# Mixer stage of a hybrid decoder layer written in another order: attention ahead of the values and state scans

## The chip, the cores and the metric

The kernel runs on one core of a Trainium2 chip. The time is the device time of one execution in microseconds (us). A core has five engines that follow their own instruction lists and wait for one another: TensorE (PE, with its weight loads as PEld), VectorE (DVE), ScalarE (ACT), GpSimd (POOL) and SyncE (SP), which here only issues DMAs.

## The reference, cut to what matters

512 tokens of width 1024 pass through a SwiGLU block, a mixer and a second SwiGLU block, all in float32, each with a norm ahead and behind. The change is in the mixer:

```python
proj = rms_norm(x, mix_pre_g) @ w_in          # q, k, v, u: 512 columns each
# attention: 4 heads, 2 components of 64, value width 128, causal
p = softmax(where(causal, q @ k.T * 64 ** -0.5, -inf))     # per head and component
o_att = rms_norm((p[0] - lam * p[1]) @ v, sub_g) * (1 - lam_init)
# state space: 32 groups of 16 channels, 64 complex states each
states = associative_scan(a_bar, b_bar @ u)   # along the 512 tokens
y = c_re @ states.real - c_im @ states.imag + d * u
g = gelu(y)
o_ssm = rms_norm(g * sigmoid(g @ w_glu + b_glu), norm_g)
x = x + rms_norm(concat(o_att, o_ssm) @ w_out, mix_post_g)
```

## The kernel before

**Products.** A float32 product is made of three matmuls of 128x128 by 128x512 (`mm3`, L150 to L152). Each weight tile is loaded by SP into `raw`, rounded by ACT into a high half `wh` (L125), and subtracted into a low half `wl` on DVE, or in this stage on POOL (L126). The tiles `raw`, `wh` and `wl` lie in a few slots that are used in turn, so the load of a later tile waits until an earlier one's low half is made.

**The mixer.** After the first SwiGLU block the inputs u of the state space are projected (`ps_u`), then query and key of head 0 (`ps_q`, `ps_k`). The states (`ssm_states`, L737 to L766) work on four blocks of eight groups: PE makes `ps_s`, DVE rotates it (`tcos`, `tsin`), POOL adds (`z`), DVE scans `z` along 64 chunks of 8 tokens (`w`), DVE and POOL rotate back (`wcos`, `wsin`), and DVE adds into `xt`. The outputs (`ssm_outputs`, L776 and L780) multiply the loaded tables `om` and `mm` with `xt` and `u` into `ps_y`, and ACT takes its gelu into `g`. The gate (`glu`) multiplies `g` with `w_glu`, whose weights are two tiles.

**Attention.** A query is split into halves (L854, L855), a key likewise (ACT L865 and L866, DVE L867, once for each of two components). Then for each block of 128 queries: scores of both components (`ps_sc`, L878 to L880; each is 128 queries by 128 to 512 keys), their maxima on DVE (`mx`), exp on ACT (`att`, L883), the difference of both on DVE, transposes back (`ps_at`, L895, copied by ACT L897), the product with the values (`ps_o`, L904), a norm (`att_n`, L915: ACT L167, DVE L160, POOL L161, DVE), and transposes (`ps_ot`, L925) into the operand of the output product. `ps_at`, `ps_ot`, `ps_y` and other small tiles share two banks of the accumulator memory, so a `ps_at` can wait for a gelu that empties its bank.

**Order.** Within the mixer PE's order is that of the code; the other engines are ordered by a scheduler at build time, and each works through its list in order. Before the attention loop the kernel writes the outputs' loads, head 0's projections, the four state blocks and the values in this order:

```python
    ssm_load_outputs()
    drain(att_query(0, xn))
    drain(att_key(0, xn))
    for b in range(4):
        ssm_states(b)
    att_values(xn)
```

The loop `attention(fill)` goes over 4 heads of 4 blocks and takes pieces of other work from the generator `fill` between its steps, as much as `HEAD_PADS` and `PADS` say. There `fill` gives the other heads' projections merged with the state space's outputs and gate (`LENS` are the lengths by which the two streams are kept level), then the first 28 steps of the output product `acc` (`w_out`).

## Time and profile before

| | |
|---|---|
| median of 3 runs | 988.95 us (987.87 to 989.09) |
| span of the profiled execution | 988.8 us |
| its own time beside the span | nothing lies around the span that a row shows: the median is 0.15 us above it |
| PE busy | 956.1 us (97%) |
| mixer, from the first `ps_u` to the last `acc` | 393 to 620 us |
| mean granted clock of TensorE | 0.990 |

The profile is one execution. A wait is put down to the instruction that released it. A granted clock of 1.00 is TensorE's level of 2.4 GHz, 0.50 that of 1.2 GHz; a stretch at 0.50 counts as busy though its matmuls take twice as long, so the busy share alone does not show it.

### The profile page before, as it was taken

To read this page: it belongs to the slowest core of one execution; us is meant where nothing else is said; L and a number is where in the kernel's file an instruction comes from. 1 tells how busy PE (TensorE), PEld (TensorE's weight loads), DVE (VectorE), ACT (ScalarE), POOL (GpSimd) and SP (SyncE) were. 2 spreads that over 40 slices of the span, in tenths; PEclk is the share of its full clock that TensorE was granted. 3 is DMA by queue.
4 is the path that set the end of the run, shared out by engine and by line. 5 is a ranking of instruction groups with operands and counts; after the bars stand their busy time and mean duration, and the time that the engine had idled before them with its cause. 6 is when DMAs were issued, how large, how long until landed. Compare 5 with 4: busy or idle time off the path is not lost.

```text
span 988.8 us, 12741 instructions
## 1 busy us (share of the span) xinstructions
PE 956.1 (97%) x4931; PEld 791.5 (80%) x4931; DVE 471.4 (48%) x946; ACT 339.4 (34%) x567; POOL 157.3 (16%) x216
## 2 busy tenths in 40 slices
PE   5999999999999999998899899999999999999997
PEld 4988777788888888986677677988888888888886
DVE  5599877633331325447467657623333333322323
ACT  5423333323221334222577545522223232312221
POOL 2105333100000033236234315000000000000000
PEclk9999999999999999999899899999999999999999
DMA  7535543533323261596211205322333333232312
GB/s 226 166 92 153 163 131 109 152 97 95 107 86 107 86 192 50 212 195 141 65 43 43 86 23 169 107 64 86 107 87 104 93 99 104 88 107 85 107 43 86
DMA packets 146172, 107.70 MB, mean 109 GB/s; under 512 B 15568, under 2 KB 126704, under 8 KB 145344
## 3 DMA queue, kind: packets, MB, share of 16 engines
q1 hardware_dynamic: 143776, 100.93, 34.8%
q0 software_dynamic: 1184, 3.87, 1.4%
q10 hardware_dynamic: 1152, 2.10, 0.6%
q8 instruction: 39, 0.64, 0.3%
q14 instruction: 21, 0.17, 0.1%
HBM read 97.99 MB, written 8.88 MB: 108 GB/s over the span
## 4 chain that ended last, share of the span: by engine, by line
PE 48%; ACT 1%; DVE 1%; issue 1%; DMA 1%; POOL 0%; DVEq 0%; POOLq 0%; ACTq 0%
PE ps_gu L152 8%; PE ps_gu L150 8%; PE ps_gu L151 8%; PE acc L152 5%; PE acc L150 5%; PE acc L151 5%; PE ps_sc L879 1%; PE ps_o L904 1%; PE ps_sc L878 1%; PE ps_y L776 1%; PE ps_k L150 1%; PE ps_sc L880 1%; DMA raw<-in_ff_w_gate_dram 1%; PE ps_k L151 0%; PE ps_q L150 0%
## 5 line engine op out<-in xcount | busy, mean ns | idle before, releaser
L125 ACT CAST wh<-raw 128x1024 fp32r<-128x1024 f32 x150 | 157.7, 1053 | 448.5 <-issue 152.9
L126 DVE TENSOR_TENSOR wl<-raw,wh 128x1024 fp32r<-128x1024 f32 x132 | 164.1, 1246 | 249.2 <-ACT wh L125 245.1
L150 PE MATMUL ps_gu<-xn_hi,wh 128*128 128x512 f32 (+1 forms) x696 | 265.3, 382 | 0.0
L151 PE MATMUL ps_gu<-xn_lo,wh 128*128 128x512 f32 (+1 forms) x696 | 265.2, 381 | 0.0
L152 PE MATMUL ps_gu<-xn_hi,wl 128*128 128x512 f32 (+1 forms) x696 | 264.9, 381 | 0.0
L150 PEld LDWEIGHTS ps_gu<-xn_hi,wh 128*128 128x128 f32 x696 | 130.8, 188 | 25.4 <-issue 0.8
L152 PEld LDWEIGHTS ps_gu<-xn_hi,wl 128*128 128x128 f32 x696 | 130.8, 188 | 25.0
L151 PEld LDWEIGHTS ps_gu<-xn_lo,wh 128*128 128x128 f32 x696 | 131.0, 188 | 24.7
L150 PE MATMUL acc<-wh,h 128*128 128x512 f32 x352 | 136.9, 389 | 0.0
L151 PE MATMUL acc<-wl,h 128*128 128x512 f32 x352 | 136.9, 389 | 0.0
L152 PE MATMUL acc<-wh,h 128*128 128x512 f32 x352 | 136.1, 389 | 0.0
L319 DVE TENSOR_TENSOR hf<-sg,ps_gu 128x512 f32<-128x512 f32 x44 | 30.2, 686 | 105.8 <-PE ps_gu L152 105.1
L150 PEld LDWEIGHTS acc<-wh,h 128*128 128x128 f32 x352 | 66.1, 188 | 13.8
L152 PEld LDWEIGHTS acc<-wh,h 128*128 128x128 f32 x352 | 66.1, 188 | 13.6
L151 PEld LDWEIGHTS acc<-wl,h 128*128 128x128 f32 x352 | 66.1, 188 | 13.6
L281 POOL TENSOR_SCALAR ss<-ss_post 128x1 f32<-128x1 f32 x12 | 2.6, 213 | 457.8 <-ACT junk_post L167 457.8
L126 POOL TENSOR_TENSOR wl<-raw,wh 128x1024 fp32r<-128x1024 f32 x18 | 44.1, 2456 | 52.8 <-ACT wh L125 52.7
L321 ACT CAST h<-hf 128x512 fp32r<-128x512 f32 x44 | 27.3, 621 | 36.6 <-DVE hf L319 30.0
L322 DVE TENSOR_TENSOR h<-hf,h 128x512 fp32r<-128x512 f32 x44 | 30.1, 684 | 1.4 <-ACT h L321 1.4
L190 PE MATMUL ps_xn<-ident,xs 128*128 128x128 f32 x96 | 14.9, 299 | 13.7 <-DVE xs L185 12.1
L167 ACT ACTIVATE junk_post<-acc 128x512 bf16<-128x512 f32 x24 | 14.3, 596 | 40.1 <-PE acc L152 39.9
L317 ACT ACTIVATE sg<-ps_gu 128x512 f32<-128x512 f32 x44 | 25.8, 587 | 1.5 <-PE ps_gu L152 1.5
(283 smaller groups left out, 1220.4 us busy)
## 6 DMA issues: line engine op xcount, KB each, us to landing
raw<-in_ff_w_gate_dram SPq DMA_DIRECT2D x44, 512.0 KB, 3.9
raw<-in_ff_w_up_dram SPq DMA_DIRECT2D x44, 512.0 KB, 3.9
raw<-in_ff_w_down_dram SPq DMA_DIRECT2D x44, 512.0 KB, 3.3
raw<-in_w_in_dram SPq DMA_DIRECT2D x16, 512.0 KB, 4.1
raw<-in_w_out_dram SPq DMA_DIRECT2D x8, 512.0 KB, 3.3
im_d<-itca SPq DMA_DIRECT2D x4, 512.0 KB, 5.0
om_d<-taps SPq DMA_DIRECT2D x4, 512.0 KB, 3.7
im<-im_d SPq DMA_DIRECT2D x2, 1024.0 KB, 10.2
```

The lines of the kernel that those rows point to most:

```text
L125: act.copy(wh, raw)
L126: eng.tensor_tensor(wl, raw, wh.bitcast(F32), ALU.subtract)
L150: pe.matmul(ps, a[0], b[0], start=start, stop=False)
L151: pe.matmul(ps, a[0], b[1], start=False, stop=False)
L152: pe.matmul(ps, a[1], b[0], start=False, stop=stop)
L167: sum_sq.ins = act.activation(into, src, AF.Square, scale=scale, accum_out=s).ins
L190: pe.transpose(ps[:, k * P:(k + 1) * P], xs[h][:, k * P:(k + 1) * P], ident)
L317: act.activation(sg, ps_g, AF.Silu)
L319: dve.tensor_tensor(hf, sg, ps_u, ALU.mult)
L321: act.copy(hi, hf)
L322: dve.tensor_tensor(lo, hf, hi.bitcast(F32), ALU.subtract)
L776: pe.matmul(ps[par * 64:par * 64 + 64, g * 64:(g + 1) * 64], lhs, rhs[:, g, par], start=(g == n == 0), stop=(g == 7 and n == 1), skip_grou ...
```

## The change

The outputs' loads, the values and the state blocks move into `fill`: the values (now token block by token block, `ps_v`, in place of a product that keeps all four token blocks open) are merged with the states, then come the outputs' loads, head 1's projections, and heads 2 and 3 merged with the outputs and the gate. The first scores are issued right behind key 0. A scan runs over four groups at once, with a `decay` tile (made by ACT, and zeroed by POOL at each group's first chunk) as its factor: 8 scans of 128x256 in place of 32 of 128x64. The last head's blocks go from the longest to the shortest. A pad that overshoots is now carried on to the next. Two scratch tiles for norm sums become one, and comments go, so lines move by 2 to 9.

```diff
-PADS = (2.4, 0.8, 0, 1.65)
+PADS = (0.7, 0.3, 0, 1.65)
-LENS = (31.2, 26.4)
-HEAD_PADS = (2.05, 0.85, 1.0, 0.6)
+LENS = (21.8, 4.6, 20.8, 26.4)
+HEAD_PADS = (9.1, 5.2, 5.2, 5.0)
...
+        decay = small.tile([P, 4, NC], F32, tag="decay", name="decay", bufs=1)
+        act.copy(decay, S.r8[:, gs].unsqueeze(2).broadcast_to([P, 4, NC]))
+        pool.memset(decay[:, :, 0:1], 0.0)
         for ri in range(2):
-            for g in range(4):
-                cs = slice(g * NC, (g + 1) * NC)
-                dve.tensor_tensor_scan(w[:, ri, cs], S.r8[:, blk * 4 + g:blk * 4 + g + 1].broadcast_to([P, NC]),
-                                       z[:, ri, cs], 0.0, ALU.mult, ALU.add)
+            dve.tensor_tensor_scan(w[:, ri, :], decay.rearrange("p g c -> p (g c)"), z[:, ri, :], 0.0,
+                                   ALU.mult, ALU.add)
...
     def att_values(xn):
-        A.v = page([P, NT, HEADS * VD], F32, "v")
...
-        drain(row_steps(xn.get, w_in, KD, 1024, outer(KD, 2), keep_v))
...
+        for t in range(NT):
+            ps = bank("acc", "ps_v")
+            for f in range(KD):
+                hi, lo = xn.get(f, t * P, (t + 1) * P)
+                wh, wl = (w[:, f % 2, :] for w in units[f // 2])
+                mm3(ps, (hi, lo), (wh, wl), f == 0, f == KD - 1)
+                yield 0.68
+            act.copy(A.v[:, t, :], ps)
+            A.v_ready.add(t)
...
     def attention(fill):
+        due = [0.0]
+
         def pad(us):
-            while us > 0:
+            due[0] += us
+            while due[0] > 0:
                 cost = next(fill, None)
                 if cost is None:
                     return
-                us -= cost
-
-        blocks = [(h, i) for h in range(HEADS) for i in range(NT)]
+                due[0] -= cost
+
+        blocks = [(h, i) for h in range(HEADS) for i in (range(NT) if h < HEADS - 1 else reversed(range(NT)))]
...
-    ssm_load_outputs()
+    att_start()
     drain(att_query(0, xn))
     drain(att_key(0, xn))
-    for b in range(4):
-        ssm_states(b)
-    att_values(xn)
...
+    def ssm_first():
+        for b in range(4):
+            ssm_states(b)
+            yield 0.9
+        ssm_load_outputs()
...
     def fill():
-        yield from merged((LENS[0], projections()), (LENS[1], ssm_rest()))
+        yield from merged((LENS[0], att_values(xn), 0.0), (LENS[1], ssm_first(), 0.2))
+        yield from projections((1,))
+        yield from merged((LENS[2], projections(range(2, HEADS)), 0.0), (LENS[3], ssm_rest(), 0.0))
```

What the change makes of the engines' lists is shown at three places. The first is PE behind the last product of key 0 (`ps_k`); before, the first state block and the values (`acc`) stand there:

```order
L150 MATMUL ps_k_3590<-xn_hi,wh 128x512
L151 MATMUL ps_k_3590<-xn_lo,wh 128x512
L152 MATMUL ps_k_3590<-xn_hi,wl 128x512
L737 MATMUL ps_s<-u,im 64x64 x32
L150 MATMUL acc<-wh,xn_hi 128x512
L151 MATMUL acc<-wl,xn_hi 128x512
```

With the change the scores of block 0 (both components) stand directly behind the key's last matmul, and the values (`ps_v`) behind them:

```order
L152 MATMUL ps_k_3571<-xn_hi,wl 128x512
L887 MATMUL ps_sc<-k,q 128x256
L888 MATMUL ps_sc<-k,q 128x256
L889 LDWEIGHTS identb
L889 MATMUL ps_sc<-cmask,identb 128x128
L887 MATMUL ps_sc<-k,q 128x256
L888 MATMUL ps_sc<-k,q 128x256
```

Moved: the scores of head 0's first block are ahead of the values and of every state block.

The second is SP's list of DMAs from the inputs u of the state space on. Before, it reads:

```order
L726 DMA u<-ud 16x16x64 x8
L700 DMA om<-om_d 128x2048
L705 DMA mm<-kd 16x16x128
L726 DMA u<-ud 16x16x64 x8
L705 DMA mm<-kd 16x16x128 x7
L700 DMA om<-om_d 128x2048
L705 DMA mm<-kd 16x16x128 x8
L138 DMA raw<-in_w_in_dram 128x8x128
L138 DMA raw<-in_ssm_w_glu_dram 128x2x512 x2
```

With the change three weight loads of `w_in` and the first of the gate's stand ahead of the tables, and the gate's second behind them:

```order
L726 DMA u<-ud 16x16x64 x16
L138 DMA raw<-in_w_in_dram 128x8x128 x3
L138 DMA raw<-in_ssm_w_glu_dram 128x2x512
L700 DMA om<-om_d 128x2048
L705 DMA mm<-kd 16x16x128 x8
L700 DMA om<-om_d 128x2048
L705 DMA mm<-kd 16x16x128 x8
L138 DMA raw<-in_ssm_w_glu_dram 128x2x512
```

Moved: the tables `om` and `mm`, from between the loads of u to behind four weight loads, and one gate load from beside the other to behind all tables.

The third is PE at the end of the last head. With the change its last three blocks stand there, block 2 of 4, then block 1, then block 0, `acc` being steps of the output product:

```order
L150 MATMUL acc<-wh,o_att 128x512
L151 MATMUL acc<-wl,o_att 128x512
L152 MATMUL acc<-wh,o_att 128x512
L904 MATMUL ps_at<-ident,att 128x128 x2
L934 MATMUL ps_ot<-ident,att_n 128x128
L913 MATMUL ps_o<-v,att 128x128 x2
L904 MATMUL ps_at<-ident,att 128x128
L934 MATMUL ps_ot<-ident,att_n 128x128
L913 MATMUL ps_o<-v,att 128x128
L934 MATMUL ps_ot<-ident,att_n 128x128
L150 MATMUL acc<-wh,o_att 128x512
```

Before, the last transposes (`ps_ot`) of that head have steps of the output product ahead of them and behind them that need only the state space (`o_ssm`):

```order
L925 MATMUL ps_ot<-ident,att_n 128x128
L904 MATMUL ps_o<-v,att 128x128 x4
L150 MATMUL acc<-wh,o_att 128x512
L151 MATMUL acc<-wl,o_att 128x512
L152 MATMUL acc<-wh,o_att 128x512
L150 MATMUL acc<-wh,o_att 128x512
L151 MATMUL acc<-wl,o_att 128x512
L152 MATMUL acc<-wh,o_att 128x512
L150 MATMUL acc<-wh,o_ssm 128x512
L151 MATMUL acc<-wl,o_ssm 128x512
L152 MATMUL acc<-wh,o_ssm 128x512
L925 MATMUL ps_ot<-ident,att_n 128x128
```

Moved: the steps of the output product that stood between the last two blocks now stand ahead of them.

## Rows read from the trace of the kernel before

**Rows 1.** The page's first part: busy time of each engine, share, instructions.
```profile
PE 956.1 (97%) x4931; PEld 791.5 (80%) x4931; DVE 471.4 (48%) x946; ACT 339.4 (34%) x567; POOL 157.3 (16%) x216
```

**Rows 2.** PE's waits at 421 to 590 us: total us, times, longest.
```profile
PE ps_sc L878 <- DVE tsin L746: 3.2, 1, 3.2
PE ps_sc L878 <- ACT att L883: 2.9, 1, 2.9
PE ps_sc L879 <- DVE k L867: 0.8, 1, 0.8
PE ps_o L904 <- ACT att L897: 0.8, 1, 0.8
```

**Rows 3.** The same view for 393 to 421 us.
```profile
PE ps_xn L190 <- DVE rinv_post L158: 1.5, 1, 1.5
```

**Rows 4.** Busy time by stretch; last three columns: clock, DMA share, GB/s.
```profile
463.30:466.70 3.40, 3.40 (x36) 2.60 (x35) 2.91 (x5) 0.00 (x0) 2.77 (x2) 0.50 0.03 7
...
562.20:565.70 3.50, 3.50 (x10) 2.67 (x10) 1.55 (x6) 0.46 (x2) 0.32 (x2) 0.51 0.17 64
```

**Rows 5.** The same columns while om and mm are loaded.
```profile
432.00:446.00 14.00, 14.00 (x170) 11.58 (x171) 12.50 (x30) 5.22 (x8) 7.06 (x8) 1.00 1.00 179
```

**Rows 6.** The timeline behind key 0: start, duration, engine, line, operation.
```profile
430.22 0.39 PE L152 MATMUL ps_k<-xn_hi,wl 128*128 128x512 f32 x1
...
431.58 0.39 PE L152 MATMUL ps_k<-xn_hi,wl 128*128 128x512 f32 x1
431.83 1.04 ACT L125 CAST wh<-raw 128x1024 fp32r<-128x1024 f32 x1 [4.39 <-PE ps_k L151]
...
435.14 0.68 DVE L867 TENSOR_TENSOR k<-ps_k,k 64x512 fp32r<-64x512 f32 x1
```

**Rows 7.** The timeline behind key 3.
```profile
556.13 0.40 PE L152 MATMUL ps_k<-xn_hi,wl 128*128 128x512 f32 x1
...
561.69 0.38 PE L879 MATMUL ps_sc<-k,q 64*128 64x256 f32 x1 [0.84 <-DVE k L867]
```

**Rows 8.** The state work by tile: durations min/median/max in ns.
```profile
L754 DVE TENSOR_TENSOR_SCAN w<-r,z x32: 256/260/2431, 436.6 to 467.2; 128x64 f32<-128x64 f32 x32
...
L746 DVE TENSOR_TENSOR tsin<-ps_s,phases x4: 681/681/692, 433.7 to 461.5; 128x512 f32<-128x512 f32 x4
...
L748 POOL TENSOR_TENSOR z<-tcos,tsin x4: 731/737/771, 435.3 to 462.3; 128x256 f32<-128x256 f32 x4
...
L759 POOL TENSOR_TENSOR wsin<-w,phases x4: 1273/1724/1749, 438.2 to 467.6; 128x512 f32<-128x512 f32 x4
...
L765 DVE TENSOR_TENSOR xt<-wcos,wsin x8: 402/418/2636, 441.3 to 472.3; 64x252 f32<-64x252 f32 x8
```

**Rows 9.** The maxima of the scores at two widths: busy us, mean ns.
```profile
L882 DVE TENSOR_REDUCE mx<-ps_sc 128x1 f32<-128x512 f32 x8 | 5.4, 687 | 1.9 <-PE ps_sc L880 1.8
...
L882 DVE TENSOR_REDUCE mx<-ps_sc 128x1 f32<-128x128 f32 x8 | 2.1, 288 | 2.5 <-PE ps_sc L880 2.5
```

**Rows 10.** SP's issue of the mm tables in the timeline.
```profile
437.56 8.69 SPq L705 DMA_DIRECT2D mm<-kd  x8
```

**Rows 11.** DMA issues at 385 to 500 us: size, median us to landing.
```profile
om<-om_d SPq DMA_DIRECT2D x2, 1024.0 KB, 9.0
mm<-kd SPq DMA_DIRECT2D x16, 128.0 KB, 8.3
...
raw<-in_ssm_w_glu_dram SPq DMA_DIRECT2D x2, 512.0 KB, 8.4
```

**Rows 12.** The timeline behind a block's last product in head 3.
```profile
586.87 0.28 ACT L167 ACTIVATE junk_post<-ps_o 128x128 bf16<-128x128 f32 x1 [0.68 <-PE ps_o L904]
...
588.70 0.27 PE L925 MATMUL ps_ot<-ident,att_n 128*128 128x128 f32 x1
```

**Rows 13.** The low halves of weights on POOL, and gelu on ACT, by tile.
```profile
L126 POOL TENSOR_TENSOR wl<-raw,wh x18: 2364/2393/2835, 389.1 to 557.5; 128x1024 fp32r<-128x1024 f32 x18
...
L780 ACT ACTIVATE g<-ps_y x4: 597/598/598, 475.6 to 492.6; 128x512 f32<-128x512 f32 x4
```

More of the change, by code (lines that the diff above doesn't have):

```diff
@@ L95, in hybrid_layer @@
     make_causal_mask(nc, cmask, MASK)
-    junk = {tag: const.tile([P, 512], BF16, name=f"junk_{tag}") for tag in ("pre", "post")}
+    junk = const.tile([P, 512], BF16, name="junk")
     mhalf = const.tile([P, 1], F32, name="mhalf")
@@ L165, in sum_sq @@
         s = tiny(1, f"ss_{tag}", bufs=4)
-        into = junk["pre" if tag[:3] == "pre" else "post"][:, 0:src.shape[1]]
+        into = junk[:, 0:src.shape[1]]
         sum_sq.ins = act.activation(into, src, AF.Square, scale=scale, accum_out=s).ins
@@ L832, in hybrid_layer, with att_start @@
     A.q, A.k, A.pg, A.po, A.on, A.pq = {}, {}, {}, {}, {}, {}
-    def att_values(xn):
-        A.v = page([P, NT, HEADS * VD], F32, "v")
-        def keep_v(t, ps):
-            act.copy(A.v[:, t, :], ps)
-        drain(row_steps(xn.get, w_in, KD, 1024, outer(KD, 2), keep_v))
+    def att_start():
         A.sub = const.tile([P, VD], F32, name="subln")
@@ L844, in att_values @@
         dve.tensor_scalar(A.sub, A.sub, 1.0 - LAM_INIT, None, ALU.mult)
-        A.o, A.out = [], set()
+        A.o, A.out, A.v_ready, A.done = [], set(), set(), {h: 0 for h in range(HEADS)}
+        A.v = page([P, NT, HEADS * VD], F32, "v")
+    def att_values(xn):
+        units = [weights(w_in[0, j * 256:(j + 1) * 256, 1024:1536].rearrange("(f p) c -> p f c", p=P), [P, 2, 512])
+                 for j in range(KD // 2)]
+        for t in range(NT):
[7 more added lines that the diff above has]
+            A.v_ready.add(t)
     def att_query(h, xn):
@@ L898, in att_mix @@
         yield
-        if i == 0:
+        if h not in A.po:
             A.po[h] = bank("acc", "ps_o")
@@ L907, in att_norm @@
     def att_norm(h, i):
-        if i == 0:
+        if h not in A.on:
             A.on[h] = scratch([P, SEQ], F32, "att_n")
@@ L919, in att_out @@
             A.pq[h] = bank(name="ps_ot")
-        if h % 2 == 0 and blocks[0] == 0:
+        if len(A.o) == h // 2:
             A.o.append(page([P, 2, 2, SEQ], F32R, "o_att"))
@@ L925, in att_out @@
             pe.transpose(A.pq[h][:, vs], A.on[h][:, vs], ident)
-        if blocks[-1] == NT - 1:
+        A.done[h] += len(blocks)
+        if A.done[h] == NT:
             A.out.add(h)
@@ L933, in merged @@
     def merged(*streams):
-        at = [0.0] * len(streams)
+        at = [s[2] for s in streams]
         live = set(range(len(streams)))
@@ L967, in attention @@
                 pad(hp * PADS[1])
+                while i not in A.v_ready:
+                    next(fill)
                 for o in out_due:
@@ L1050, in __getitem__, with projections @@
             return w_out[b, r0:r0 + 256, cols]
-    def projections():
-        for h in range(1, HEADS):
+    def projections(heads):
+        for h in heads:
             yield from att_query(h, xn)
             yield from att_key(h, xn)
+    def ssm_first():
[3 more added lines that the diff above has]
+        ssm_load_outputs()
     def ssm_rest():
```

## The prediction

> **What bounds the kernel now.** The page comes first: PE is busy 956.1 us, 97% of the span [rows 1], so a change can pay only where PE waits or runs slowly, or cost where it makes PE do so. The second view is that of PE's waits in the stretches that the change touches. From 421 us to the end of attention PE waits 3.2 us for `tsin`, the second rotation of the last state block, 2.9 us for an exp, and twice 0.8 us behind key 3 [rows 2]; a small transposing step at 396 us waits 1.5 us for a norm [rows 3]. These make 9.2 us. The third view is the granted clock by stretch. It falls to 0.50, the 1.2 GHz level, in four stretches, of which the first and the last are shown [rows 4]; their lengths are 3.4, 6.9, 3.5 and 3.5 us, 17.3 us at half speed, so some 8.6 us are lost in them. Each followed waits of about 1 to 3 us. All that the change could win is thus about 18 us, half of it only if the clock stays up.
>
> **What the change takes away.** The 3.2 us for `tsin` went because the scores of head 0 stood behind all values and met the last state block's work on DVE; in the new order three of four blocks' work lies under the values. The 2.9 us for exp has the same root. The two waits of 0.8 us behind key 3 fall away as such and come back below in another size. At 396 us the new order gives the norm more products to hide under, so I take the 1.5 us as gained too. Sum: 9.2 us.
>
> **The scans.** The scan of 128x64 takes 0.26 us [rows 8], so a 128x256 costs at most four of these, 1.04 us. From below, DVE's maxima take 687 ns at 512 columns and 288 ns at 128 [rows 9], 1.04 ns a column; 192 more columns add 0.20 us, 0.46 us in all. I take 0.7 us; eight of them make 5.6 us in place of 8.3 us. Nearly all of it is off PE's path. [...] No row of before shows a long scan. [...] The four copies that make `decay` go to ACT and four small memsets to POOL, where there is idle time; they cost nothing unless that cover goes, and then some 0.6 us each, the nearest row being a key cast of half a microsecond's size.
>
> **New wait A: scores right behind key 0.** Before, a state block and the values covered the splitting of the key. Now PE's last key matmul is followed by the scores. In the trace the last key matmul starts at 431.58, ACT rounds a weight tile first (431.83, 1.04 us), and the first DVE low half only starts at 435.14, a cast of the query having been between [rows 6]. Behind key 3 the same chain for both components is seen in full: from the last key matmul at 556.13 to the scores that end it at 561.69 plus 0.38 are 5.9 us, with a copy of about half a microsecond between [rows 7], so 5.4 us. PE has 0.23 us of the key and 1.3 us of scores to do in that time: 3.8 us of wait. Bounds: 3 to 4.4 us.
>
> **Waits K1, K2, K3: scores behind keys 1 to 3.** In the new order only three, six and three matmuls (0.68 to 1.36 us; six matmuls start within 1.36 us [rows 6]) stand between a key and its first scores. For key 1 no weight cast is ahead: 5.4 less 1.04, less 0.23, 0.68 and 1.3 leaves 2.2 us. Key 2 has the cast ahead and six matmuls: 5.4 less 2.9, 2.5 us. Key 3 has the cast and three matmuls, and longer scores: 2.7 us. Together 7.4 us; bounds 5 to 10.
>
> **Wait E: the state chain.** DVE's list now runs the blocks strictly after one another: the rotation of block 1 stands behind the four `xt` of block 0, and the scores of block 2 wait on PE for the bank that `tsin` of state block 2 empties. One turn is two rotations (1.36 us), two `z` (1.48), a scan (0.7), `wsin` (1.5 to 1.72) and four `xt` (1.7) [rows 8], some 6.9 us. PE begins the values at zero, the first block's `tsin` ends at 7.2, the third's at about 21.5. PE gets there at 18.7 (59 matmuls, three `ps_s`, the scores). That is 3 us; bounds 1.5 with the fast scan to 4.5 with the slow one and POOL's longest `wsin`.
>
> **Wait G: the second gate tile.** SP's tables moved. The load of the first gate tile waits for a slot that POOL frees with the low half of key 1's weights, at about 33 us on the same scale (PE has reached the last quarter of the values, then 1.05 us of cast and two low halves of 2.39 us [rows 13]). Only then come `om`, eight `mm`, `om`, eight `mm`. Eight `mm` took SP 8.69 us [rows 10] while the DMA engines were busy all the time [rows 5]: the sixteen take 17.4 us, to about 51. The second gate tile is behind them and landed 8.4 us after issue before [rows 11], so it lands at about 59; bounds 55 and 60. ACT's list has its cast between two exps, and POOL's has its low half ahead of the last state block's `z`. The gelu of the first outputs waits for that block's `wcos` and `wsin`, since `g` is laid into the memory of the phases that they read. So the gelu ends a cast (1.05), a low half (2.39), two `z` (1.48), a scan (0.7), a `wsin` (1.72) and 0.6 us of gelu [rows 8, 13] later, 8 us: at 63 to 68. PE needs the gelu's bank for the transposes of head 0's last block. It is there at 56 if the clock stays up, at about 61 if waits A, E and K1 each bring a half-speed stretch of 3.4 us like those of before. Hence 2 to 12 us; I take 7. Behind the waiting cast on ACT stand the second exp of head 1's first block and all gelus, and PE waits for those next.
>
> **Tail T.** The last head's two shortest blocks now stand at the end with no step of the output product between them. The norm from a block's last product to its transposes takes 1.83 us (586.87 to 588.70) [rows 12]. The end is a copy (0.5), a norm, transposes, another norm, and the halves of the last transposes before the output product can go on, since its next step needs token block 0: 0.5 plus 1.8 plus 1.8 plus some 0.6. That is 4.5 us (bounds 3 to 5.5) where before steps of the output product lay between.
>
> **Sum.** 3.8 + 7.4 + 3.0 + 7 + 4.5 = 25.7 us of new waits, less 9.2 gained: 16.5 us. The half-speed time I leave as it is, 8.6 us: new waits of 2 to 7 us are no shorter than those that it followed before. From the profiled 988.8 us, 0.15 us under the median, this gives **1005 us**; the bounds of the terms reach from 996 to 1015.
>
> **Rivals.** *G and E vanish.* If the tables' load keeps up, because less else loads beside it, and the state chain is shorter, the sum is 15.7 less 9.2: 995 us (990 to 996). For it: the first gate tile and three weights no longer share the DMA with the tables at the same moment. Against: the DMA share of 1.00 [rows 5].
> *Faster, by the clock.* The granted clock stays at 2.4 GHz through the new waits. That gives back 8.6 us, so the kernel is faster as soon as the new waits sum to under 17.8 us, which they do without G and with E or K a little smaller: 15.7 less 17.8 is -2, some 986 us. For it: the wait in the tail of before, under a microsecond, brought no half-speed stretch. Against: four longer ones did [rows 4].
> *Waits only move.* New and old waits balance, 989 us: then A and K would have to cost a third of what key 3's chain shows [rows 7].
> *More half-speed time.* Each new wait of over 2 us brings a stretch and G is at its long end: 1018 us.
>
> **How the numbers follow.** The forecast has a chance of 0.50. G and E vanish: 0.19. Faster: 0.17. Balance within 0.2%, about what a measurement of this kernel can tell from no change: 0.06. More half-speed time: 0.08. Slower is thus 0.77. The range from 986 to 1016 us leaves out the far ends of the last rival and of the faster one.
>
> **What the profile after would show.** PE waiting for `k` (the low halves) behind each key, 2 to 4 us each; for `tsin` once, some 3 us; for the gelu `g` at a `ps_at`, with the second gate tile landing late and ACT waiting for its DMA; for `att_n` at the end of head 3, twice. The 1.5 us at 396 us gone. I would be wrong if the key waits are under 1.5 us each, if the gelu wait is absent, or if no stretch of the mixer is at 1.2 GHz.

## The result, and the profile after

The changed kernel takes **1042.74 us** (four runs, 1041.62 to 1047.65) against 988.68 us of the kernel before measured beside it (987.87 to 989.09): a ratio of 1.0553 [1.0525, 1.0582]. It is 54 us slower. The prediction was 1005 us with a range of 986 to 1016: the sign was right, the size not. The profiled execution has a span of 1041.3 us, 52.5 us more than before.

First the page: the first line answers to [rows 1], the others are PE's busy tenths and its granted clock in 40 slices of 26 us.

```profile
PE 974.4 (94%) x4931; PEld 802.7 (77%) x4931; DVE 466.0 (45%) x922; ACT 341.2 (33%) x571; POOL 157.4 (15%) x220
...
PE   6999999999999998889399797999999999999997
...
PEclk9999999999999999989799898999999999999999
```

PE has the same 4931 matmuls, but is busy 18 us longer, and the span has grown by three times that. Both the busy tenths and the clock dip in slices 16 to 25, the mixer. So the loss has two parts: time in which PE stands still, and time in which it runs at half speed. The stretch view separates them. The next two rows are the mixer from 385 us to where the second SwiGLU block begins, after and then before (PE busy, PEld, DVE, ACT, POOL, granted clock, DMA share, GB/s).

```profile
385.00:673.00 288.00, 239.18 (x1439) 188.10 (x1438) 136.61 (x270) 120.74 (x267) 88.90 (x88) 0.89 0.30 79
```

```profile
385.00:621.00 236.00, 223.80 (x1453) 179.32 (x1453) 142.81 (x296) 120.09 (x265) 88.85 (x85) 0.96 0.39 105
```

PE idles 48.8 us (288 less 239.18) in place of 12.2. Busy time times one less the clock, summed over stretches of 1 us each, gives what half speed costs: 23.2 us in place of 8.3. That is 36.6 and 14.9 us more, 51.5 in all. The way from 385 us to the first matmul of the second SwiGLU block is 52.5 us longer (to 672.9 in place of 620.4), which is the whole loss of the span: outside this stage nothing changed.

What a clock of 0.50 means is in PE's rows: a 128x512 matmul of `ps_v` starts every 0.427 us at 440.1 to 444.0 us, at 0.50, and every 0.23 us at 445.1 to 446.0 us, at 1.00. That is 1.9 times as long and not twice, so the reckoning by the clock puts the loss a little high. By columns, 512 in 0.427 us are 1.2 per ns at 0.50; at 1.00 256 more of them cost 0.107 us (0.227 us for 512 in `ps_k` [rows 6], 0.120 us for 256 in the `ps_u` of before), 2.4 per ns. Levels of 1.2 and 2.4 GHz are an estimate from these rows, if a column is one cycle.

Where PE idles, the chain of waits says by name (393 to 680 us; total us, times, longest). It answers to [rows 2] and [rows 3].

```profile
PE ps_at L904 <- ACT g L782: 14.2, 1, 14.2
PE ps_sc L887 <- ACT k L875: 7.2, 8, 2.1
PE ps_sc L887 <- DVE rinv_att L160: 4.6, 1, 4.6
PE ps_u L150 <- ACT xn_hi L193: 4.3, 1, 4.3
PE ps_z L150 <- DVE q L864: 4.2, 1, 4.2
PE ps_ot L934 <- DVE att_n L924: 3.4, 2, 1.7
PE ps_os L823 <- DVE og L819: 2.6, 1, 2.6
PE ps_sc L888 <- DVE k L876: 2.6, 8, 0.5
PE ps_gt L798 <- ACT g L782: 1.3, 1, 1.3
```

None of the waits of [rows 2] and [rows 3] is left in its place; the 1.2 us for an exp stand at 631 us, in the last head. The predicted ones are all here: `g` (G), `k` in sixteen pieces (A and K), `att_n` twice (T), and one of 4.6 us (E). Two things were not predicted: 4.3 us for `xn_hi` at the very start, where a gain was expected, and the gate's waits (`ps_z`, `ps_os`, `ps_gt`), 9.1 us in all with one of 1.0 for `gl`.

**Behind key 0** (answers to [rows 6]):

```profile
433.39 0.39 PE L152 MATMUL ps_k<-xn_hi,wl 128*128 128x512 f32 x1
435.92 0.39 PE L887 MATMUL ps_sc<-k,q 128*128 128x256 f32 x1 [2.14 <-ACT k L875]
436.64 0.38 PE L888 MATMUL ps_sc<-k,q 64*128 64x256 f32 x1 [0.33 <-DVE k L876]
...
437.84 0.46 PE L887 MATMUL ps_sc<-k,q 128*128 128x256 f32 x1 [0.66 <-ACT k L875]
438.57 0.58 PE L888 MATMUL ps_sc<-k,q 64*128 64x256 f32 x1 [0.27 <-DVE k L876]
```

The four brackets make 3.4 us. The last matmul takes 0.58 us where the same form took 0.38 before it: the clock has fallen (0.50 from 438.0 us on). By stretch, behind keys 0 and 1 (answers to [rows 4]):

```profile
440.00:444.00 4.00, 4.00 (x11) 3.03 (x11) 0.96 (x4) 0.19 (x2) 0.00 (x0) 0.50 0.05 14
...
495.00:499.00 4.00, 2.08 (x17) 1.22 (x18) 1.85 (x4) 2.15 (x5) 0.00 (x0) 1.00 1.03 252
499.00:503.00 4.00, 4.00 (x61) 3.14 (x59) 0.11 (x1) 0.00 (x0) 0.00 (x0) 0.57 1.21 149
```

PE is busy all the time there, at a clock of 0.50 throughout behind key 0 and for most of the 4 us behind key 1 (0.57). Behind keys 2 and 3 (557 to 561 and 605 to 609 us) the clock is 0.57 too. Behind key 1 PE stood still for 0.57, 0.33, 0.67 and 0.34 us, in the 4 us of the second row, still at 1.00: no single wait was longer than 0.7 us, and the clock fell all the same.

**E.** The wait of 4.6 us is put down to `rinv_att`, an instruction of 0.14 us. The first of the rows below shows the likelier releaser: `tsin`, which by the code empties the bank for the scores, ends at 465.70, 0.14 us ahead of them.

```profile
465.02 0.68 DVE L746 TENSOR_TENSOR tsin<-ps_s,phases 128x512 f32<-128x512 f32 x1
...
465.84 0.66 PE L887 MATMUL ps_sc<-k,q 128*128 128x384 f32 x1 [4.56 <-DVE rinv_att L160]
```

**G**, in order of time: SP's issues, then the gate's second tile through ACT and POOL, the last state block, the gelu and PE (answers to [rows 10], [rows 11] and [rows 13]).

```profile
481.41 0.42 SPq L700 DMA_DIRECT2D om<-om_d  x1
481.93 8.80 SPq L705 DMA_DIRECT2D mm<-kd  x8
...
492.65 9.69 SPq L705 DMA_DIRECT2D mm<-kd  x8
503.26 0.40 SPq L138 DMA_DIRECT2D raw<-in_ssm_w_glu_dram  x1
...
510.55 1.04 ACT L125 CAST wh<-raw 128x1024 fp32r<-128x1024 f32 x1 [12.61 <-DMA raw<-in_ssm_w_glu_dram]
...
511.67 2.34 POOL L126 TENSOR_TENSOR wl<-raw,wh 128x1024 fp32r<-128x1024 f32 x1 [18.15 <-ACT wh L125]
...
517.52 1.28 ACT L782 ACT_TABLE_LOAD   x1 [5.58 <-DVE wcos L760]
518.82 0.60 ACT L782 ACTIVATE g<-ps_y 128x512 f32<-128x512 f32 x1
...
519.47 0.90 PE L904 MATMUL ps_at<-ident,att 128*128 128x128 f32 x3 [14.18 <-ACT g L782]
```

The chain is the one that was predicted, link by link. SP takes 21.9 us from the first `om` to the second gate tile, ACT waits 12.6 us for that tile, and PE stands from 505.3 to 519.5 us.

**The scan** (by tile; min/median/max in ns), to be read against [rows 8]:

```profile
L756 DVE TENSOR_TENSOR_SCAN w<-decay,z x8: 659/672/1200, 451.1 to 516.0; 128x256 f32<-128x256 f32 x8
```

0.66 to 0.67 us, where 0.7 was taken between the 0.46 us from the slope of the maxima [rows 9] and the 1.04 us of four short scans [rows 8].

**The start of the stage**, where 1.5 us were to be won:

```profile
387.01 5.52 POOL L126 TENSOR_TENSOR wl<-raw,wh 128x1024 fp32r<-128x1024 f32 x2
...
390.23 2.85 DVE L288 SCALAR_TENSOR_TENSOR x<-half,rinv_post,x 128x512 f32<-128x512 f32 x1
...
393.17 0.63 ACT L167 ACTIVATE junk<-x 128x512 bf16<-128x512 f32 x1 [3.98 <-DVE x L288]
...
395.36 0.56 ACT L193 CAST xn_hi<-ps_xn 128x512 fp32r<-128x512 f32 x1
...
395.98 0.62 PE L150 MATMUL ps_u<-xn_hi,w_lead 128*128 128x256 f32 x3 [4.27 <-ACT xn_hi L193]
```

ACT now has two norm sums (`junk`), which both need a late `x`, ahead of the `xn_hi` that PE wants. `x` is late because its addition took 2.85 us, where the next one of its kind took 0.74: it began under POOL's low halves and ended 0.5 us behind the second of them. Two products with a gain (`xs`) ahead of it in DVE's list took 3.55 us under the same low halves. In the kernel before two such products took 1.41 us with no low half on POOL, and 5.75 us from 394.6 us on, where POOL made low halves for 4.95 us of that time. Why, no run tests. The wait of 1.5 us in [rows 3] is gone; in the trace of before it stands at 398.9 to 400.5 us, not at 396.

**The gate and the tail.** `ps_z` needs a bank that the second half of head 3's query frees late, and the last two norms of head 3 stand open, of which the first is shown (answers to [rows 12]):

```profile
577.98 0.69 DVE L864 SCALAR_TENSOR_TENSOR q<-ps_q,q 64x512 fp32r<-64x512 f32 x1
...
578.81 0.76 PE L150 MATMUL ps_z<-wh,gh 128*128 128x512 f32 x1 [4.15 <-DVE q L864]
...
639.70 0.48 PE L934 MATMUL ps_ot<-ident,att_n 128*128 128x128 f32 x1 [1.67 <-DVE att_n L924]
```

### The profile page after: what moved, and what is told of

It reads as the page before. It is cut to its first block, busy times and chain, and to the rows that moved or that the text cites. A ratio compares the mean times of both kernels' runs of the same rounds, so it can differ in the third digit from the quotient of the medians.

```text
span 1041.3 us, 12724 instructions
## 1 busy us (share of the span) xinstructions
PE 974.4 (94%) x4931; PEld 802.7 (77%) x4931; DVE 466.0 (45%) x922; ACT 341.2 (33%) x571; POOL 157.4 (15%) x220
## 4 chain that ended last, share of the span: by engine, by line
PE 69%; DVE 7%; DMA 4%; ACT 3%; issue 2%; POOL 2%; SPq 0%; DVEq 0%; POOLq 0%; ACTq 0%
PE ps_gu L150 11%; PE ps_gu L151 11%; PE ps_gu L152 11%; PE acc L150 8%; PE acc L152 8%; PE acc L151 8%; DMA mm<-kd 2%; PE ps_sc L888 1%; PE ps_u L151 1%; ACT junk L167 1%; PE ps_u L152 1%; PE ps_o L913 1%; PE ps_u L150 1%; PE ps_v L150 1%; DMA raw<-in_ssm_w_glu_dram 1%
## 5 line engine op out<-in xcount | busy, mean ns | idle before, releaser
L167 ACT ACTIVATE junk<-acc 128x512 bf16<-128x512 f32 x24 | 14.3, 597 | 39.9 <-PE acc L152 39.7
L887 PE MATMUL ps_sc<-k,q 128*128 128x256 f32 (+2 forms) x32 | 13.4, 420 | 13.0 <-ACT k L875 7.2
```

The source lines that it names most:

```text
L167: sum_sq.ins = act.activation(into, src, AF.Square, scale=scale, accum_out=s).ins
L887: pe.matmul(ps[:, 0:m], q[:, c, ts], k[:, c, 0:m], start=True, stop=False)
```

## The experiments

A kernel is the changed one with the edit shown, unless the kernel before is named. Ratios are against the kernel before on the same chip; "less" means less than the 1042.7 us of the changed kernel. The median of the kernel before went from 987.3 to 989.9 us over these chips, and the intervals of e1, e3, e4, e5, e9, e10 and e18 overlap that of the changed kernel (e16's touches it, with both its runs below the four there): the times of those seven show no difference from it, and what they show is read from the waits in one profiled execution each.

### The gelu's wait, G

**e3: both gate tiles ahead of the tables.** Their loads become a function of their own, called ahead of `ssm_load_outputs()`.

```diff
-    def glu_init():
+    def glu_weights():
...
+
+    def glu_init():
...
+        glu_weights()
```

> The changed kernel with both tiles of the gate's weights loaded ahead of the tables om and mm. Theory (the 14.2 us wait for the gelu's bank is the late landing of the second gate tile, passed on by the lists of ACT and POOL): that wait falls to under 4 us, the tables come some 2 us later and add a wait of 0 to 4 us at ps_y, and the kernel is 8 to 14 us faster, about 1031. Rival (the gelu waits for the last state block's chain whatever the load does): under 4 us faster.

1039.12 us, ratio 1.0523 [1.0463, 1.0583]. The wait for `g` fell only from 14.2 to 10.6 us, for ACT met the next load behind the tables instead:

```profile
505.25 1.04 ACT L125 CAST wh<-raw 128x1024 fp32r<-128x1024 f32 x1 [9.45 <-DMA raw<-in_w_in_dram]
```

So it is not the gate tile in particular: the load that comes next behind the tables is late.

**e4: the page of `g` taken ahead of the phases,** so that the gelu need not wait for the last state block's `wcos` and `wsin`.

```diff
+        S.g = page([P, 4, SW], F32, "g")
...
-        S.g = page([P, 4, SW], F32, "g")
```

> The changed kernel with the memory of g given out ahead of that of the phases, so that g is not laid into the phases. Theory (the late second gate tile holds ACT's list until its cast, and the chain behind it over z, scan and wsin to the gelu is only there because g shares the phases' memory): the wait at ps_at falls from 14.2 to about 7 us, the time by 5 to 8 us to about 1036. Rival (the chain is not what the gelu waits for): unchanged within 2 us.

1043.54 us, 1.0568 [1.0537, 1.0598]; the wait was 15.2 us. `g` was laid into the same memory again (the gelu still waits for `wcos`), so the edit did not do what it was meant to: inconclusive.

**e5: the page of `g` claimed early,** by which it does lie elsewhere.

```diff
-        S.g = page([P, 4, SW], F32, "g")
+        S.g = claim(page([P, 4, SW], F32, "g"))
```

> The changed kernel with g laid into memory of its own (91008 in place of the phases' 99200), so that a gelu no longer overwrites what the last state block reads; nothing is left out. Theory (14.2 us of wait = about 7 us for the late gate tile, passed on because its cast is ahead in ACT's list, and about 7 us of chain over z, scan and wsin that only the shared memory adds): the wait at ps_at falls to 5 to 9 us and the time by 5 to 9 us. Rival (the late gate tile alone): unchanged within 2 us.

1038.97 us, 1.0511 [1.048, 1.0542].

```profile
PE ps_at L904 <- ACT g L782: 8.5, 1, 8.5
```

The shared memory costs 5.7 of the 14.2 us. The remaining 8.5 is the cast in ACT's list that waits for its load.

**e16: plain tables.** The `mm` tables are read as one DMA of 1 MB each out of the `om` tables, in place of eight with short pieces. It leaves out the true values of `mm`.

```diff
-            for tau in range(TC):
-                sp.dma_start(out=tv[tau * CH:(tau + 1) * CH],
-                             in_=kd[:, j * 16:j * 16 + 16, 112 - 16 * tau:240 - 16 * tau])
+            sp.dma_start(out=t, in_=S.om_d[:, 2 * j:2 * j + 2, :])
```

> The changed kernel with each mm table read by one plain DMA of 1 MB out of the om table in place of eight that cut it out of another tensor in pieces of 512 bytes; it leaves out the true values of mm, and no other work. Theory (the 14.2 us at ps_at are the sixteen mm loads of about 1.1 us each ahead of the second gate tile in SP's list): the second gate tile is issued within some 12 us of the first om in place of 22 and is waited for less, the wait at ps_at falls to 2 to 7 us, and the kernel is 8 to 14 us faster. Rival (what is waited for is the state chain and the lists of ACT and POOL, not the load): under 3 us faster.

1032.67 us, 1.0453 [1.0357, 1.0548]: 10 us less.

```profile
PE ps_at L902 <- ACT g L780: 3.6, 1, 3.6
```

```profile
483.61 0.42 SPq L700 DMA_DIRECT2D om<-om_d  x1
...
485.60 0.47 SPq L138 DMA_DIRECT2D raw<-in_ssm_w_glu_dram  x1
...
500.62 1.05 ACT L125 CAST wh<-raw 128x1024 fp32r<-128x1024 f32 x1 [0.51 <-DMA raw<-in_ssm_w_glu_dram]
```

SP passes the tables in 2 us in place of 21.9, and ACT waits 0.5 us for the gate tile in place of 12.6. The tile itself now takes 15 us from its issue to the cast, in place of 7.3, so the cast comes 12.1 us sooner behind the first `om` and not 19.9. What is left, 3.6 us, is the chain of the last state block to the gelu. The place of G, its price and the part of the short pieces in it are shown. Whether SP's issuing or the DMA engines set the pace is not separated, but the rows speak for the engines: they are busy all the time in both kernels (share 1.10 and 1.00), at 200 GB/s in the changed one (481 to 503.3 us) and 362 GB/s here (483.6 to 500.6 us). In e2, where nothing else loads beside the first eight `mm`, SP is through with them in 3.8 us, and the engines are still busy behind it (449 to 455 us: share 1.26 at 122 GB/s).

### The keys' waits and the clock

**e2: a cover behind each key,** six pieces of other work ahead of each head's first scores.

```diff
+                fresh = n == 0
                 while blocks[n][0] not in A.ready:
                     next(fill)
+                    fresh = True
+                if fresh:
+                    for _ in range(6):
+                        next(fill)
                 att_scores(*blocks[n])
```

> The changed kernel with six more pieces of other work (about 4 us) between each key and its first scores. Theory (waits stand alone, each costs its length and the half-speed stretch behind it): the 9.8 us that PE waits for k nearly go, and with some 5 us of half-speed time the kernel is 10 to 15 us faster, about 1030. Rival (the wait only moves: ACT and DVE set the pace, or the pieces taken early are missing later): under 5 us faster.

1020.02 us, 1.0329 [1.0299, 1.0359]: 22.7 us less, with e11 below the largest gain of a single edit. The waits for `k` were gone but for 0.7 us, but so was nearly all of G:

```profile
PE ps_at L904 <- ACT g L782: 1.7, 1, 1.7
```

The cover also moves the tables ahead of the third weight load and both gate loads in SP's list (`mm` issued from 447 us on, in place of 482). Idle time fell to 31.2 us, the loss to half speed to 17.7 us.

**e6: PE kept busy where it waits,** by matmuls of constants whose result is overwritten. By the condition chosen they stood ahead of the first two blocks of each head, not of one.

```diff
+            if h not in A.po:
+                for _ in range(36 if c == 0 else 14):
+                    pe.matmul(ps[:, 0:P], identb, cmask, start=True, stop=True)
             pe.matmul(ps[:, 0:m], q[:, c, ts], k[:, c, 0:m], start=True, stop=False)
```

> The changed kernel with 36 and 14 matmuls of 128 columns (cmask and identb into the score's own bank, overwritten by the score) ahead of the first scores of each head, on PE only; they fill the waits for the key and add no wait. Theory (of the clock: the half-speed stretches behind keys 0 to 3 come from PE standing still): waits for k fall in the rows but the scores start no sooner, the stretches at 1.2 GHz behind the four keys go, and the kernel is 4 to 8 us faster. Rival (the clock has another cause): within 2 us, or slower by what the matmuls overrun.

1049.58 us, 1.0618 [1.0592, 1.0644]: slower. The clock from 433 to 444 us was 1.00 and the loss to half speed 15.9 us in place of 23.2, but the second set had no wait to hide in and cost its own length, some 3.1 us in each head.

**e18: the same ahead of one block only.**

```diff
+            if i == (0 if h < HEADS - 1 else NT - 1):
+                for _ in range(36 if c == 0 else 14):
+                    pe.matmul(ps[:, 0:P], identb, cmask, start=True, stop=True)
```

> As e6, but with the 36 and 14 matmuls only ahead of the first block of each head; in e6 they stood ahead of the second block's scores as well, where PE waits for nothing, and cost there about 3 us a head. Theory (the half-speed stretches behind the keys come from PE standing still): 1.2 GHz goes behind keys 0, 1, 2 and 3, the scores start within 1 us of where they did behind their keys, and the kernel is 3 to 7 us faster than the changed one. Rival (keeping PE busy gives nothing back): within 2 us, or slower.

1040.55 us, 1.0512 [1.0441, 1.0582]. The stretches behind keys 0 and 1, as above:

```profile
440.00:444.00 4.00, 3.66 (x27) 2.84 (x28) 1.92 (x7) 3.17 (x7) 0.38 (x1) 1.00 0.45 131
499.00:503.00 4.00, 4.00 (x72) 3.10 (x71) 0.29 (x1) 0.00 (x0) 0.00 (x0) 1.00 1.24 143
```

Behind keys 2 and 3 the clock is 1.00 as well, and so it is at 444 to 447 us. The scores begin 2.5 us behind key 0 in both kernels, with the same chain through ACT and DVE, and only here does PE work through most of it (waits of 0.62, 0.33 and 0.34 us are left); the clock then stays at 1.00. The loss to half speed is 16.3 us, 6.9 less: the four stretches (8.4 us by the same reckoning) are gone, and one of 1.7 us at 663 us is new. The time shows no clear gain. In this execution key 0 came 3.3 us later, 2.1 of them ahead of the first `ps_u` and so ahead of any filler; nine of head 0's fillers ran at 414 us already. From key 0 on to the second SwiGLU block it took 235.2 us in place of 239.5, 4.3 less. So each key's waits do bring a stretch at half speed; 2.6 of the 6.9 us did not reach the end.

**e8: the cover in the kernel before.**

```diff
             if n < len(blocks):
+                if n == 0:
+                    for _ in range(6):
+                        next(fill)
```

> The kernel before with six pieces of the other work (about 5 us) taken ahead of the first scores, where PE waits 3.2 us for tsin and 2.9 us for an exp and then runs at 1.2 GHz. Theory (waits stand alone and bring the half-speed stretches): the 3.2 us go, the clock stays up there, and the kernel is 4 to 9 us faster than before, about 982. Rival (the first state outputs and query 1 are not ready either, or the exp's wait grows): within 2 us of before.

996.7 us, 1.0085 [1.0065, 1.0105]: slower. The waits of [rows 2] for `tsin` and exp were gone, but others took their place:

```profile
PE ps_y L776 <- ACT g L780: 5.3, 1, 5.3
PE acc L150 <- DVE k L867: 3.2, 1, 3.2
```

My theory, that the old waits were there for the taking, falls. It fits that in the kernel before they stand where the outputs and the keys would be late otherwise, but no run tests that.

### The start of the stage, and the scans

**e7: the kernel before with one scratch tile for norm sums.**

```diff
-    junk = {tag: const.tile([P, 512], BF16, name=f"junk_{tag}") for tag in ("pre", "post")}
+    junk = const.tile([P, 512], BF16, name="junk")
...
-        into = junk["pre" if tag[:3] == "pre" else "post"][:, 0:src.shape[1]]
+        into = junk[:, 0:src.shape[1]]
```

> The kernel before with one scratch tile for all norm sums in place of two, and nothing else of the change. Theory (the two 4.3 us that PE waits for xn_hi at 391 us come from the other order that the scheduler makes of this stage when the two tiles are one): PE waits 4.3 us there in place of 1.5, a half-speed stretch follows, and the kernel is 3 to 5 us slower, about 993. Rival (that wait belongs to the moved loads and weights): within 1 us of before.

991.62 us, 1.004 [1.0025, 1.0055]: 4.1 us slower, and the wait is the one of the changed kernel:

```profile
PE ps_u L150 <- ACT xn_hi L193: 4.3, 1, 4.3
```

The small edit alone makes it. With one tile each norm sum overwrites the last one's scratch, and the scheduler put ACT's list in another order. The wait of 1.5 us of [rows 3] is gone here too, without the new order.

**e9: the changed kernel with the old 32 scans and two scratch tiles** (the change undone in these two places; the tiles by e7's lines the other way round).

```diff
-            dve.tensor_tensor_scan(w[:, ri, :], decay.rearrange("p g c -> p (g c)"), z[:, ri, :], 0.0,
-                                   ALU.mult, ALU.add)
+            for g in range(4):
+                cs = slice(g * NC, (g + 1) * NC)
+                dve.tensor_tensor_scan(w[:, ri, cs], S.r8[:, blk * 4 + g:blk * 4 + g + 1].broadcast_to([P, NC]),
+                                       z[:, ri, cs], 0.0, ALU.mult, ALU.add)
```

> The changed kernel with the 32 scans of 128x64 and the two scratch tiles of before. Theory (the one scratch tile costs some 4 us at 391 us with its half-speed stretch, and the two long scans save 2 times 0.4 us on DVE in each state block): PE's 4.3 us wait for xn_hi falls to 1.5, the wait for the state chain grows from 4.6 to about 5.5, and the kernel is 2 to 4 us faster. Rival (the long scans are what the new order lives on): slower than the changed kernel.

1040.53 us, 1.0528 [1.0448, 1.0608]: no difference that the times show. The wait for `xn_hi` was gone, that of 1.5 us for a norm was back (1.6 us), and E stayed at 4.5 us and G at 15.0. The scans decide nothing that shows, one way or the other.

### The tail

**e1: the last head's blocks from the shortest to the longest again.**

```diff
-        blocks = [(h, i) for h in range(HEADS) for i in (range(NT) if h < HEADS - 1 else reversed(range(NT)))]
+        blocks = [(h, i) for h in range(HEADS) for i in range(NT)]
```

> The changed kernel with the last head's blocks from the shortest to the longest again. Theory (the tail's 5.2 us of waits behind two norms are the price of the reversed order, with a half-speed stretch behind them): waits for att_n at the end of head 3 fall from 3.4 to under 1.5 us and the time falls by 3 to 6 us, to about 1038. Rival (the longest block last has a longer exp and difference chain, and the waits only change their name): within 1.5 us of the changed kernel.

1045.03 us, 1.0583 [1.0552, 1.0613]. PE waits 3.5 us for `att_n`, as much as with the reversed order. So the reversed order is not the tail's cause.

**e10: less of the output product spent early in the last head.**

```diff
-HEAD_PADS = (9.1, 5.2, 5.2, 5.0)
+HEAD_PADS = (9.1, 5.2, 5.2, 3.6)
```

> The changed kernel with 3.6 in place of 5.0 as the last head's pad, so that two steps of the output product stand between the last blocks and two behind them, where before there were none. Theory (the tail's 5.2 us come from the output product's steps being used up, not from the reversed blocks): the waits for att_n at the end fall from 3.4 to about 1 us and the kernel is 3 to 5 us faster. Rival (the waits only move to the earlier blocks of head 3): within 1.5 us.

1041.29 us, 1.0536 [1.0474, 1.0598]: no gain that shows. One wait of 2.7 us for `att_n` was left, and the wait for a weight's low half (`wl`) had grown from 0.6 to 2.1 us.

### The pads

**e11: the pads of the kernel before,** in the new order.

```diff
-PADS = (0.7, 0.3, 0, 1.65)
+PADS = (2.4, 0.8, 0, 1.65)
...
-HEAD_PADS = (9.1, 5.2, 5.2, 5.0)
+HEAD_PADS = (2.05, 0.85, 1.0, 0.6)
```

> The changed kernel with the pads of before (PADS 2.4, 0.8, 0, 1.65 and HEAD_PADS 2.05, 0.85, 1.0, 0.6): less other work between the steps of one block, more left for later. Theory (the waits for keys are there because a key's scores come at once when the projection ends, whatever the pads): the waits for k stay within 2 us of 9.8, the gelu's wait changes with what stands ahead of it, and the time stays within 10 us of the changed kernel. Rival (the large pads are the whole loss): within 10 us of the kernel before.

1019.96 us, 1.032 [1.0232, 1.0408]: 22.8 us less, though the waits behind the keys stayed:

```profile
PE ps_sc L887 <- ACT k L875: 7.4, 8, 2.1
PE ps_os L823 <- DVE og L819: 4.7, 1, 4.7
```

The tables are issued from 454 us on, again ahead of the third weight load and the gate loads, and G is gone. The gate still waits (9.2 us with one of 3.7 and one of 0.8). In the tail the waits for `att_n` are 1.2 us in place of 3.4, with the last head's order reversed as before this edit.

**e14: old pads, and the projections of all heads merged with the gate,** so that the gate's steps stand further apart.

```diff
-        yield from projections((1,))
-        yield from merged((LENS[2], projections(range(2, HEADS)), 0.0), (LENS[3], ssm_rest(), 0.0))
+        yield from merged((31.2, projections(range(1, HEADS)), 0.0), (LENS[3], ssm_rest(), 0.0))
```

> The changed kernel with the pads of before and with the projections of all three later heads merged with the state space's outputs and gate, as before the change, so that more matmuls lie between two steps of the gate. Theory (the new waits of 10 us at ps_gt, ps_z and ps_os are there because two heads' projections in place of three lie between the gate's steps): those waits fall under 4 us against 9.2 with the pads alone, and the time falls below 1015. Rival (they come from ACT's and DVE's lists, whatever is merged): those waits stay over 7 us.

1015.69 us, 1.0263 [1.0193, 1.0333]: 4 us less than e11, within what the two intervals allow by chance. The gate waits 6.0 in place of 9.2 us.

### What is left of the order itself

**e12: e2's cover, e5's claim, e9's scans and tiles, and a last pad of 3.0.** No line is new but the pad.

> The changed order with all that the runs so far point to: six pieces between a key and its scores, g in memory of its own, two scratch tiles and the short scans, and a last pad of 3.0 that leaves steps for the end. Theory (waits are separate terms): from 1020 us of the covered keys another 3 us for the scratch tiles and 4 us for the tail, about 1012. Better than before only if the half-speed time falls below 10 us: under 990, which I give one chance in ten. Rival (ACT's and DVE's lists set the pace and take the gains back): 1018 or more.

1019.99 us, 1.0321 [1.0248, 1.0393]. No better than the cover alone: what the others take away comes back as waits of `ps_o` for `att` (5.5 us) and `acc` for `k` and `wl` (4.5 us).

**e13: e11's pads, e2's cover, e9's scans and tiles.**

> The changed order with the pads of before, six pieces between a key and its scores, and the scratch tiles and short scans of before. Theory (the wait for the gelu is decided by where in the work the tables' loads fall, which the pads set, and the key waits are separate): from the 1020 us of the pads alone another 9.6 us of key waits, their half-speed stretches and 3 us of the scratch tiles come off, about 1003. Rival (the covers take the same work from elsewhere): 1015 or more.

1018.19 us, 1.0288 [1.0222, 1.0354]. The two edits that each gave some 22.7 us give 24.6 together. Alone, each had moved the tables forward in SP's list and taken G away; together they do not keep that place: here the first `om` is issued at 470 us, behind three weight loads. A wait of `ps_y` for `g` (5.0 us) was new, and waits for `k` were back (4.2 and 2.9 us).

**e15: e13 and e14's merging.** Of the change the order is left: attention first, values (token block by token block) with states, outputs behind, and the last head reversed, and with it the pad that is carried on. The key cover is added.

> The changed order of attention, values and states (and the reversed last head) with pads, merging, scratch tiles and scans of before and the key cover. Theory (each of these is a term of its own): about 995, the rest being the state chain and one or two half-speed stretches. Rival (the order itself costs): 1005 or more.

1013.43 us, 1.024 [1.0158, 1.0322].

```profile
PE ps_y L777 <- DMA mm<-kd: 10.8, 1, 10.8
PE ps_sc L886 <- DVE rinv_att L160: 4.1, 1, 4.1
```

Still 24 us slower than before. The outputs now wait for the tables themselves, which SP issues from 467 us on, in the kernel before from 422. Ahead of them SP waits 33.5 us for a low half (`wl`) with the second gate load, which stands ahead of the tables here, and passes on to the first `om` at once:

```profile
467.27 0.42 SPq L700 DMA_DIRECT2D om<-om_d  x1
```

The memory that the tables take can hold them too: in e2 SP waits 13.2 us for `ps_s`, the product of the states, ahead of `mm`. In e15 no such wait shows.

**e17: e15 with e16's plain tables** (again without the true values of `mm`).

> The kernel with all restored but the order of attention, values and states, with the same plain loads of the mm tables (their true values are left out). Theory (its 10.8 us wait at ps_y for mm is the price of the order, since the tables' memory comes free only behind the states): that wait falls under 3 us and the kernel is 8 to 13 us faster, about 1002. Rival (the wait only moves to the state chain or the gate): under 4 us faster.

1006.15 us, 1.0184 [1.0117, 1.0252].

```profile
PE ps_y L775 <- DMA mm<-om_d: 4.5, 1, 4.5
```

This is less than the 8 to 13 us of the theory and more than the rival's 4: the wait for `mm` is 6.3 us shorter, the time 7.3 us (5.5 by the two ratios). So some 6 of those 24 us are the tables' short pieces. No version was faster than the kernel before.

## Why the prediction was wrong in size

The sum's terms against the rows of after, in us of PE standing still:

| term | predicted | measured |
|---|---|---|
| A, key 0 | 3.8 | 3.4 |
| K1 to K3 | 7.4 | 6.4 (9.8 in all `k` rows, less A) |
| E, state chain | 3.0 | 4.6 |
| G, gelu | 7 | 14.2 |
| T, tail | 4.5 | 3.8 (`att_n` 3.4, `o_att` 0.4) |
| idle time of before, taken off | -9.2 | -12.2 (all of it) |
| start, for `xn_hi` | a gain, in the line above | 4.3 |
| gate | none | 9.1 |
| rest, the 1.2 for an exp among it | none | 3.0 |
| half speed | 0 | 14.9 |
| sum | 16.5 | 51.5 |

**A, K and T** came out as worked out, each inside its bounds; they were read from chains that the trace of before held in full [rows 7, 12]. That T is caused by the reversed order did not hold: e1 has the same waits with the old order, and e11 has 1.2 us of them with the reversed one. What opens the tail is rather the pads, which leave no steps of the output product there; keeping some of them (e10) brought another wait.

**The half-speed time was the largest miss.** The step that failed is "The half-speed time I leave as it is, 8.6 us". It was argued from a remark on the length of the waits, which says nothing of their number: each key's waits brought a stretch of their own. It is 23.2 us, 14.9 more than the 8.3 of before. The four stretches behind the keys make 8.4 us of it, and e18 shows their cause. The others follow the start (1.7 us), E (3.0), G (1.9), the gate's waits (4.1) and those in the last head (3.8) in the trace, which no experiment separated. The rival "more half-speed time" had the mechanism, but at 1018 us a size of about half and a chance of 0.08.

**G was the right chain with two terms mis-sized.** From the values' start (439.1) the step had the tables begin at about 33 and end at 51; they began at 42.3 and ended at 64.1. The beginning was late because it hangs on PE's progress through the values, and in the 42 us up to 481 PE lost 4.6 us to E and some 5.6 us to half speed (37.4 us busy at a mean clock of 0.85), losses of the same sum that I had not carried into the next term. The passage took 21.9 us in place of 17.4 because the `mm` issues took 8.8 and 9.7 us, against 8.69 in [rows 10], with gaps of about a microsecond at each `om`, which the sum had left out. The landing of 7.3 us and the chain behind the cast, 8.9 us with an activation table load of 1.28 us that I had left out, were close to 8.4 and 8. PE, itself delayed, came at 66 in place of 56 to 61. That leaves 14.2 us, 2.2 over the long bound. e16 shows the passage's part (10.6 us less wait), e5 the memory's (5.7); together they are more than 14.2, so they overlap.

**E** had turns of 6.9 us; they were 8.9 and 7.6 (`tsin` ends at 449.3, 458.1 and 465.7). In the first turn some 3 us of softmax work stand in DVE's list, which the new order puts there and the sum did not count; the second has none. The first `tsin` ended 10.1 us behind the values' start in place of 7.2, the third at 26.6 in place of 21.5 (7.2 and two turns of 6.9 make 21.0). PE came at 22.1 in place of 18.7, delayed mainly by the stretch at half speed behind key 0. That the wait is only 1.6 us over the forecast is partly luck: two misses of 5.1 and 3.4 us, one against the other.

**The start.** "I take the 1.5 us as gained too" came true by luck, and cost more than it gave. The sentence looked at the products that the new order puts there and not at the scratch tile, which the change also takes away and which the text ahead only mentions in passing. The one tile takes the 1.5 us away (e7; with two tiles they are back in e9) and brings the 4.3 us. e7 prices it alone: 4.1 us.

**The gate.** Its waits were in no step. The change drops the sharing between gate and projections of three heads to two (`LENS`), so the gate's steps follow one another closer, and the halves of head 3's query and the gate's own products queue on ACT and DVE. e14 fits it (9.2 to 6.0 us), but its time is not told apart from e11's, so this cause is argued rather than shown.

**The scan** was right: the 0.7 us were a choice between two bounds, as no row of before has a long scan; the changed kernel took 0.66 to 0.67 us, and it decides nothing (e9).

What stays open: e15 is still 24 us slower. PE stands still for 30.1 us there, in place of 12.2 before, and loses 11.7 us to half speed, in place of 8.3. Of the 30.1 us 10.8 are for the tables and 4.1 for the state chain; the rest are small waits that change place from version to version. Whether the tables could be loaded earlier with all else put back was not tried.

## What to carry to other kernels

When each new wait on the bounding engine comes by itself, price it twice: its length, and the stretch at the lower clock behind it (here 3.4 us of waits behind key 0, and 6.8 us at a clock of 0.50 from 438.0 us on). When a term hangs on another engine's progress, carry the delays of the earlier terms into it before comparing arrival times. And go through every allocation that a change touches, also a scratch tile or a page: an order written for one place is remade by the scheduler everywhere that memory is shared.

## What the runs showed of the hardware that I had not expected

- Short waits were followed by the lower clock. Behind key 0 PE stood still four times, 2.14, 0.33, 0.66 and 0.27 us, and the clock was 0.86 for those 7 us and 0.50 for the next 4. Behind key 1 the four waits were 0.57, 0.33, 0.67 and 0.34 us, and the clock was 1.00 for those 4 us and 0.57 for the next 4. With constant matmuls in the same places (e18) it was 1.00 throughout, though the scores behind key 0 began as late.
- Eight DMAs of 128 KB that gather short pieces took SP 8.8 to 9.7 us to issue in the changed kernel, behind a table of 1 MB each, and 3.7 to 3.8 us in e2, where no other load was under way; a plain megabyte as one DMA took 0.4 us (e16).
- A DVE addition of 0.74 us took 2.85 us under two POOL subtractions, and two products of 1.41 us together took 3.55 us.
